# First attention's last quarter: transposes moved from TensorE to DMA, and their joins placed in the output projection

## The chip, the cores and the metric

The program runs on one core of one Trainium2 chip. The metric is the device time of one execution in microseconds, as the median of several runs.

## The reference

Two decoder layers over 256 tokens of 1024 features in float32. Layer 0 mixes tokens with a dilated sliding-window attention, layer 1 with a forgetting attention, and a gated feed-forward network follows each. What matters here is layer 0's mixer: three groups of 16 heads of 64 features (windows of dilation 1, 4 and 16), whose softmaxes are merged by their denominators, and the output projection behind it:

```python
def dilated_mixer(h, w_in, w_out):
    proj = (h @ w_in).reshape(B, S, N_GROUPS, 3, N_HEADS, HEAD_DIM)
    for g, (window, dil) in enumerate(DILATED_PATTERNS):
        q = partial_rotary(proj[:, :, g, 0], pos)
        k = partial_rotary(proj[:, :, g, 1], pos)
        v = proj[:, :, g, 2]
        o, lse = dilated_band_attention(q, k, v, dil, window // dil)
    ...
    wts = jax.nn.softmax(jnp.stack(lses, axis=0), axis=0)
    o = jnp.einsum('gbsh,gbshd->bshd', wts, jnp.stack(outs, axis=0))
    return o.reshape(B, S, ATTN_WIDTH).astype(h.dtype) @ w_out
```

## The kernel before

**Arithmetic.** Each float32 matrix product is made of three multiplications (`mm3`): operands are split into a high half (written by ScalarE, L80) and a low half (the rest, by VectorE, L84), and high x high, high x low and low x high are added in PSUM. I call the three together a product. Weights arrive in pieces of two loads of 512 KB (`raw`, five buffers, issued by SyncE at L101), and each load is split once by L80 and once by L84 into `wh` and `wl` (four buffers each). A load may be issued when the low half of the load five places earlier has been made.

**The first attention** goes over four quarters of heads (`hq` 0 to 3), each of two pairs (`pr` 0, 1) of two heads. A quarter's work is strung between the projections of the next by a table of due times (`later(i, fn, ...)`): scores, masks, softmax (`softmax_a`, in tiles `p` of 128 x 640, that is five blocks of 128 for a head), the transposing of these probabilities, and the values (`pv_a`, L313: the transposed probabilities times `v`, 24 small multiplications a pair), whose result is split into row blocks `oth`/`otl`, the input of the output projection.

The probabilities are transposed in two ways. For quarters 0 to 2, `turn_a`: GpSimd copies a head's tile so that the low 16-bit halves of all its words lie apart from the high ones (L528), a DMA issued by SyncE transposes this as ten blocks of 16-bit numbers (L530, tile `turned`), and ScalarE joins the halves again (L531). For quarter 3, `trans_a`: TensorE transposes blocks against an identity (`transposed`, L301; ten for a pair), and ScalarE and VectorE copy them out of PSUM (L306).

**The output projection** (`out_proj`) multiplies two token tiles (`t` 0, 1), with two halves of the columns (`n`) and eight row blocks (`k`): 16 products per token tile, accumulated in `ps_sc` for t = 0 and `ps_mm` for t = 1. Row blocks 6 and 7 come from quarter 3. What is still due from the attention is strung between the products of t = 0: after six products the transposes of pair 0, after three more those of pair 1, after three more the values of both pairs; then come the products of blocks 6 and 7, the residual and the norm of tile 0, and t = 1's products with the norm's transposes (L196) behind 12 of them.

**Order.** Each engine and the queue of SyncE run their instructions strictly in the order that the tile framework wrote; parts of the program under `first()` get a higher priority in it, and `tc.issue_after(x)` places instructions behind `x`. The copies of values (L285, sixteen a quarter) run on GpSimd.

Of the kernel before, what the change touches and what calls it, by code (L numbers as in the profile page):

```python
# [10 lines left out]
F32 = mybir.dt.float32  # L11
# [6 lines left out]
P = 128  # L18
D = 1024
S = 256  # L20
# [12 lines left out]
def trunk(ctx: ExitStack, tc: tile.TileContext, T, out):  # L33
# [219 lines left out]
    def p_tile(n=512, dtype=F32, name="p"):  # L253
        return ap.tile([P, 640], dtype, tag="p", name=name, bufs=6)[:, :n]

    def v_tile(o=None, r=None):

        v = ap.tile([P, 512], F32, tag="v", name="v", bufs=7)
        with first():
            if r:  # L260
                for t in range(2):
                    s = slice(t * S, (t + 1) * S)
                    nc.scalar.activation(v[:, s], o[:, s], AF.Copy, scale=r[t])
            elif o is not None:
                nc.scalar.activation(v, o, AF.Copy)
        return v
# [28 lines left out]
    copied = {}  # L295

    def transposed(blocks, copy=nc.vector.tensor_copy, tag="tr", home="pt"):

# [208 lines left out]
                    else:  # L507
                        nc.vector.tensor_scalar(s, s, f, None, op0=ALU.mult)

    def trans_a(quad, pr):  # L510

        pt = quad["pt"]
        block = lambda h, i: pt[pr, h][:, i * P:(i + 1) * P]
        home = ("pt", "bias")[pr]
        quad["w", pr] = [transposed([block(h, 1 + qb) for h in range(2) for qb in range(2)], nc.scalar.copy, home=home),
                         transposed([block(h, 3) for h in range(2)], home=home),
                         transposed([block(h, b * 4) for h in range(2) for b in range(2)], nc.scalar.copy, "o", home)]

    def turn_a(quad, pr):

        quad["w", pr] = []
        bufs = {"pt": 3, "bias": 4}
        parts = lambda x: x[:, :640].bitcast(U16).rearrange("p (c t) -> p t c", t=2)
        for h in range(2):
            home = ("pt", "bias")[pr]
            w = ap.tile([P, 640 if home == "pt" else 6 * P], F32, tag=home, name="pt", bufs=bufs[home])
            split16 = w[:, :640].bitcast(U16)
            nc.gpsimd.tensor_copy(split16.rearrange("p (t c) -> p t c", t=2), parts(quad["pt"][pr, h]))  # L528
            turned = ap.tile([P, 6 * P], F32, tag="bias", name="turned", bufs=4)[:, :640].bitcast(U16)
            nc.sync.dma_start_transpose(turned.rearrange("p (g c) -> p g c", c=P), split16)  # L530
            nc.scalar.copy(parts(w), turned.rearrange("p (t c) -> p t c", t=2))  # L531
            quad["w", pr].append(w)

    def pv_a(quad, pr):
        vs, ws = quad["v"], quad["w", pr]
        o = psum("o")
        if len(ws) == 2:
            blocks = [w[:, :640].rearrange("p (i j) -> p i j", j=P) for w in ws]
            straight = lambda h: ws[h][:, P:3 * P]
            corner = lambda h: ws[h][:, 3 * P:4 * P]  # L540
            dilated = lambda h, a: blocks[h][:, 0:5:4, a * 32:a * 32 + 32]
        else:
            straight = lambda h: ws[0][:, h * S:(h + 1) * S]
            corner = lambda h: ws[1][:, h * P:(h + 1) * P]
            dilated = lambda h, a: halves(ws[2][:, h * S:(h + 1) * S], a)
        pv(o[:, :S], vs[0], 0, pr, straight, S, True, False)
        pv(o[:, P:S], vs[0], 1, pr, corner, P, False, False)
        halves = lambda x, a: x.rearrange("p (b n) -> p b n", b=2)[:, :, a * 32:a * 32 + 32]
        for a in range(4):
            pv(halves(o[:, :S], a), vs[1 + a % 2], a // 2, pr, lambda h: dilated(h, a), 64, False, a == 3)  # L550
# [10 lines left out]
    for i, (hq, g, w) in enumerate(a_units):  # L561
# [19 lines left out]
        if w < 2:  # L581
# [26 lines left out]
            if w == 1:  # L608

                j = i + (hq == 0)  # L610
                step = lambda hq: 9 * hq + 11 + 2 * (hq == 0)
                if g == 0:
                    later(step(hq - 1) + 2 if hq else j + 3, scores_0, quad)
                if g == 2:
                    later(j + 1, scores_12, quad)
                    later(j + 1, softmax_a, quad)
                    for pr in range(2):
                        if hq == 3:
                            later(step(hq) + pr, trans_a, quad, pr)
                        else:  # L620
                            later(j + 1, turn_a, quad, pr)
                    for pr in range(2):
                        later(step(hq) + 2, pv_a, quad, pr)
        elif g == 0 and hq > 1:
# [30 lines left out]
                parts.append(sq(hn[:, s]))  # L655
        return hn, parts

    def out_proj(nm, ot, h, grow, ks, done, banks):

        ws = [weights(nm, i) for i in range(4)]  # L660
        xt = xt_tile()
        res = []

        def part(t, acc, nk):
            last = None
            for n, k in nk:
                c = (k % 2) * D + n * 512
                last = mm3(acc[n], both(ot, ALL, k, slice(t * P, (t + 1) * P)),
                           both(ws[k // 2], ALL, slice(c, c + 512)), k == 0, k == KT - 1)
            return last  # L670

        def cols(ks):
            return [(n, k) for n in range(2) for k in ks]

        for t in range(2):
            acc = [psum(banks[t]) for _ in range(2)]
            if t == 0:

                nk = cols(range(ks))
                last = part(t, acc, nk[:done])  # L680
                nk = nk[done:]
                per = -(-len(nk) // (len(due) - 1))
                for i in sorted(due):
                    with tc.issue_after(last.ins):
                        for fn, a in due[i]:
                            fn(*a)
                    last = part(t, acc, nk[:per]) or last
                    nk = nk[per:]
                due.clear()
                part(t, acc, nk)  # L690
                last = part(t, acc, cols(range(ks, KT)))
            else:
                part(t, acc, cols(range(2)))
                with tc.issue_after(last.ins):
                    part(t, acc, cols(range(2, 6)))
                    norm_t(*res[0], grow, xt, 0)
                    part(t, acc, cols(range(6, KT)))
            res.append(residual(acc, h[t], f"h_{nm}{t}"))
        return res, xt


    def ffn(l, hs, xt, grow, mid):
# [106 lines left out]
        res.append(residual(acc[1], hs[1][0], f"hf{l}1") if l == 0 else (acc[1], hs[1][0]))  # L809
        return res  # L810

    g_f = load_grow(1)
    hs, xt = out_proj("a_out", ot, x, g_f, 6, 6, ("sc", "mm"))
    cst.tile([P, P], F32, name="gap")
    bf = cst.tile([P, NH], F32, name="bf")
    nc.sync.dma_start(bf, T["bf"].partition_broadcast(P))
# [189 lines left out]
        for fn, a in due.pop(i, ()):  # L1006
            fn(*a)
    g_f = load_grow(3)
    hs, xt = out_proj("b_out", ot, [h for h, _ in hs], g_f, 6, 9, ("mm", "sc"))

    def finish(t, h, parts):
        r = rstd(parts)
# [126 lines left out]
```

## Time and profile before

| | us |
|---|---|
| median of 3 runs | 737.42 (736.22 to 738.65) |
| the profiled execution | 736.1 |
| its span, first to last instruction | 734.3 |
| TensorE busy in the span | 726.4 (99%) |
| VectorE busy | 495.9 (68%) |
| ScalarE busy | 388.7 (53%) |
| GpSimd busy | 83.0 (11%) |

The profile names engines PE (TensorE), PEld (its weight loads), DVE (VectorE), ACT (ScalarE), POOL (GpSimd) and SP (SyncE, with its DMA queue). Times in rows are microseconds from the start of the span unless marked ns. Matmuls are pipelined: how long work takes TensorE is read from one start to the next, not from a row's length. The last product of the attention's projections ends at about 225.5, and the output projection takes from there to about 253.4.

### The profile page before, as it was taken

How to read it: one execution, taken by the hardware profiler on the slowest of the kernel's cores; microseconds unless marked ns; L12 is line 12 of the kernel's file. 1: busy time of each engine (PE TensorE's matmuls, PEld its weight loads, DVE VectorE, ACT ScalarE, POOL GpSimd, SP SyncE). 2: the span in 40 equal slices, each digit the busy share in tenths (PEclk: the TensorE clock that was granted, in tenths of full speed). 3: DMA queues.
4: the chain of work that ended last, by engine and by line, in shares of the span. 5: the costliest groups of instructions: out<-in, count | busy, mean ns of one | idle time of the engine just before them, and what ended most of it. 6: DMA issues, size and time to landing. Idle time of an engine off the chain costs nothing.

```text
span 734.3 us, 14310 instructions
## 1 busy us (share of the span) xinstructions
PE 726.4 (99%) x5856; PEld 672.4 (92%) x5856; DVE 495.9 (68%) x762; ACT 388.7 (53%) x617; POOL 83.0 (11%) x118
## 2 busy tenths in 40 slices
PE   9999999999999999999999999999999999999996
PEld 7999989999988899999999989999889999999995
DVE  6997998998996775554555474576776554556533
ACT  7646747738445663444554453587475444545421
POOL 0600206007105000000000004110010000000001
PEclk9999999999999999999999999999999999999998
DMA  9865955956864376656567352874547656656601
GB/s 335 306 202 174 237 182 153 289 193 152 268 194 160 116 241 221 195 179 203 195 202 247 127 168 90 294 260 138 172 142 237 222 179 203 195 188 218 198 1 58
DMA packets 55042, 141.93 MB, mean 193 GB/s; under 512 B 20257, under 2 KB 21441, under 8 KB 54977
## 3 DMA queue, kind: packets, MB, share of 16 engines
q1 hardware_dynamic: 54832, 140.88, 59.4%
q8 instruction: 46, 0.75, 0.4%
q14 instruction: 20, 0.16, 0.1%
q10 hardware_dynamic: 144, 0.15, 0.1%
HBM read 136.00 MB, written 1.07 MB: 187 GB/s over the span
## 4 chain that ended last, share of the span: by engine, by line
PE 97%; DVE 1%; ACT 1%; POOL 0%; issue 0%; POOLq 0%; DVEq 0%; ACTq 0%
PE ps_mm L208 34%; PE ps_mm L203 17%; PE ps_tr L208 9%; PE ps_sc L208 8%; PE ps_o L208 7%; PE ps_tr L203 5%; PE ps_sc L203 4%; PE ps_o L203 4%; PE ps_o L313 2%; PE ps_sc L395 2%; PE ps_tr L196 1%; PE ps_tr L301 1%; PE ps_sc L476 1%; PE ps_o L322 1%; PE ps_sc L894 0%; PE ps_sc L458 0%
## 5 line engine op out<-in xcount | busy, mean ns | idle before, releaser
L80 ACT ACTIVATE wh<-raw 128x1024 fp32r<-128x1024 f32 x236 | 243.4, 1054 | 207.1 <-PE ps_tr L208 66.7
L84 DVE TENSOR_TENSOR wl<-raw,wh 128x1024 fp32r<-128x1024 f32 x236 | 288.3, 1242 | 82.6 <-ACT wh L80 82.4
L203 PE MATMUL ps_mm<-xt,wh 128*128 128x256 f32 x816 | 227.2, 279 | 0.2 <-ACT v L281 0.2
L208 PE MATMUL ps_mm<-xt,wl 128*128 128x256 f32 x816 | 226.0, 277 | 0.0
L208 PE MATMUL ps_mm<-xt,wh 128*128 128x256 f32 x816 | 226.0, 277 | 0.0
L203 PEld LDWEIGHTS ps_mm<-xt,wh 128*128 128x128 f32 x816 | 153.1, 188 | 2.2 <-issue 1.7
L208 PEld LDWEIGHTS ps_mm<-xt,wl 128*128 128x128 f32 x816 | 153.6, 188 | 0.1
L208 PEld LDWEIGHTS ps_mm<-xt,wh 128*128 128x128 f32 x816 | 153.4, 188 | 0.0
L208 PE MATMUL ps_tr<-xt,wh 128*128 128x256 f32 x304 | 83.9, 276 | 0.0
L208 PE MATMUL ps_tr<-xt,wl 128*128 128x256 f32 x304 | 83.9, 276 | 0.0
L203 PE MATMUL ps_tr<-xt,wh 128*128 128x256 f32 x304 | 83.7, 276 | 0.0
L730 DVE TENSOR_TENSOR sa<-ps_tr,sa 128x256 f32<-128x256 f32 x38 | 16.1, 424 | 73.5 <-PE ps_tr L208 73.5
L208 PEld LDWEIGHTS ps_tr<-xt,wh 128*128 128x128 f32 x304 | 57.1, 188 | 0.0
L208 PEld LDWEIGHTS ps_tr<-xt,wl 128*128 128x128 f32 x304 | 57.0, 188 | 0.0
L203 PEld LDWEIGHTS ps_tr<-xt,wh 128*128 128x128 f32 x304 | 57.0, 188 | 0.0
L203 PE MATMUL ps_mm<-wh,xt 128*128 128x512 f32 (+1 forms) x144 | 49.8, 346 | 0.0
L173 POOL TENSOR_SCALAR rs<-ssq 128x1 f32<-128x1 f32 x7 | 1.9, 271 | 420.6 <-ACT junk L182 420.6
L208 PE MATMUL ps_mm<-wl,xt 128*128 128x512 f32 (+1 forms) x149 | 49.1, 335 | 0.0
L208 PE MATMUL ps_mm<-wh,xt 128*128 128x512 f32 (+1 forms) x149 | 49.1, 335 | 0.0
L285 POOL COPY v<-v 32x256 f32<-32x256 f32 x64 | 40.5, 632 | 71.2 <-ACT v L281 68.6
L203 PE MATMUL ps_sc<-wh,ah 128*128 128x512 f32 x80 | 31.4, 392 | 0.0
L208 PE MATMUL ps_sc<-wl,ah 128*128 128x512 f32 (+1 forms) x82 | 31.3, 385 | 0.0
(232 smaller groups left out, 1113.6 us busy)
## 6 DMA issues: line engine op xcount, KB each, us to landing
raw<-in_gu SPq DMA_DIRECT2D x88, 512.0 KB, 4.8
raw<-in_a_in SPq DMA_DIRECT2D x68, 512.0 KB, 5.0
raw<-in_dn SPq DMA_DIRECT2D x44, 512.0 KB, 4.7
raw<-in_b_in SPq DMA_DIRECT2D x24, 512.0 KB, 5.0
raw<-in_a_out SPq DMA_DIRECT2D x8, 512.0 KB, 5.0
raw<-in_b_out SPq DMA_DIRECT2D x8, 512.0 KB, 4.4
bias<-sums SPq DMA_DIRECT2D x8, 384.0 KB, 6.6
grow<-in_norms SPq DMA_DIRECT2D x4, 512.0 KB, 5.7
```

Of the source, the lines that this page charges most:

```text
L80: a = nc.scalar.activation(view(hi), src, AF.Copy)
L84: return nc.vector.tensor_tensor(view(lo), src, view(hi).bitcast(F32), op=ALU.subtract)
L196: nc.tensor.transpose(tr[:, k * P:(k + 1) * P], xn[:, kk * P:(kk + 1) * P], ident)
L203: nc.tensor.matmul(o, sh, mh, start=start, stop=False)
L208: last = nc.tensor.matmul(o[:, u], s, m[:, u], start=False, stop=end and u.stop == n)
L285: nc.gpsimd.tensor_copy(v[1 + a % 2][n:n + 32, a // 2 * S:a // 2 * S + S], by_t[a * 32:a * 32 + 32, t, g])
L301: nc.tensor.transpose(tr[:, i * P:(i + 1) * P], b, ident)
L313: nc.tensor.matmul(o[h * HD:(h + 1) * HD], v[:, c:c + HD], w(h), start=start, stop=stop)
L322: nc.tensor.matmul(o[:, :n], mhalf.to_broadcast([P, P]), mhalf.to_broadcast([P, n]), start=True, stop=True)
L395: nc.tensor.matmul(lead[t], xt[y][:, k, t * P:(t + 1) * P], w[z][:, u], start=k + y + z == 0, stop=k == KT - 1 and z == 1)
L476: nc.tensor.matmul(sc[h][c, o:o + 64], q[HR[h], pr, qb * P + a * 32:qb * P + a * 32 + 32], k[HR[h], pr].rearrange("p (b n) -> p b n", b=2) ...
L730: nc.vector.tensor_tensor(a, u, sg, op=ALU.mult)
```

## The change

The quarter 3 of the first attention also goes through `turn_a`. Its parting copies run on GpSimd for pair 0 and on VectorE for pair 1, under `first()`. The joins are taken out of `turn_a` into `join_a`; for quarter 3 they are due at 38 and 39, in the output projection, with `tc.issue_after` the last copy of values of that quarter's own head group (`copied["v"]`, L263 before), on ScalarE for pair 0 and on VectorE for pair 1. The turned tiles get another home: for the first head of pair 1 the buffers `pt`, else `bias`. `out_proj` takes an explicit list of products that come before and between the due work: eight products of t = 0 (blocks 0 to 3), four of t = 1 (blocks 0 and 1), four of t = 0 (blocks 4 and 5), with the due work behind the fourth, the ninth and the sixteenth. The second layer's output projection passes a list that gives the same order as before.

```diff
-    def trans_a(quad, pr):
...
+    def parted(x):
+        return x.bitcast(U16).rearrange("p (c t) -> p t c", t=2)
 
     def turn_a(quad, pr):
 
-        quad["w", pr] = []
-        bufs = {"pt": 3, "bias": 4}
-        parts = lambda x: x[:, :640].bitcast(U16).rearrange("p (c t) -> p t c", t=2)
+        last = quad["hq"] == 3
+        by = (nc.gpsimd, nc.vector)[last and pr].tensor_copy
+        home = lambda tag: ap.tile([P, 640 if tag == "pt" else 6 * P], F32, tag=tag, name="pt",
+                                   bufs={"pt": 3, "bias": 4}[tag])[:, :640]
+        quad["w", pr], quad["turned", pr] = [], []
         for h in range(2):
...
-            nc.gpsimd.tensor_copy(split16.rearrange("p (t c) -> p t c", t=2), parts(quad["pt"][pr, h]))
-            turned = ap.tile([P, 6 * P], F32, tag="bias", name="turned", bufs=4)[:, :640].bitcast(U16)
-            nc.sync.dma_start_transpose(turned.rearrange("p (g c) -> p g c", c=P), split16)
-            nc.scalar.copy(parts(w), turned.rearrange("p (t c) -> p t c", t=2))
+            with first() if last else nullcontext():
+                w = home(("pt", "bias")[pr])
+                apart = w.bitcast(U16)
+                by(apart.rearrange("p (t c) -> p t c", t=2), parted(quad["pt"][pr, h]))
+                turned = home(("bias", "pt")[pr * (h == 0)]).bitcast(U16)
+                nc.sync.dma_start_transpose(turned.rearrange("p (g c) -> p g c", c=P), apart)
             quad["w", pr].append(w)
+            quad["turned", pr].append(turned)
+            if not last:
+                join_a(quad, pr, h)
+
+    def join_a(quad, pr, h, by=nc.scalar.copy):
+        with tc.issue_after(copied["v"].ins) if quad["hq"] == 3 else nullcontext():
+            by(parted(quad["w", pr][h]), quad["turned", pr][h].rearrange("p (t c) -> p t c", t=2))
...
-                        if hq == 3:
-                            later(step(hq) + pr, trans_a, quad, pr)
-                        else:
-                            later(j + 1, turn_a, quad, pr)
+                        later(j + 1, turn_a, quad, pr)
+                        for h in range(2) if hq == 3 else ():
+                            later(38 + pr, join_a, quad, pr, h, (nc.scalar.copy, nc.vector.tensor_copy)[pr])
...
-    def out_proj(nm, ot, h, grow, ks, done, banks):
+    def out_proj(nm, ot, h, grow, head, at, banks):
...
+        cols = lambda t, ks: [(t, n, k) for n in range(2) for k in ks]
+        last = None
+        for a, b in zip((0, *at), (*at, len(head))):
+            last = part(head[a:b]) or last
+            if due:
                 with tc.issue_after(last.ins):
-                    part(t, acc, cols(range(2, 6)))
-                    norm_t(*res[0], grow, xt, 0)
-                    part(t, acc, cols(range(6, KT)))
-            res.append(residual(acc, h[t], f"h_{nm}{t}"))
+                    for fn, a in due.pop(min(due)):
+                        fn(*a)
+        last = part(cols(0, range(KT)))
+        res = [residual(accs[0], h[0], f"h_{nm}0")]
+        part(cols(1, range(2)))
+        with tc.issue_after(last.ins):
+            part(cols(1, range(2, 6)))
+            norm_t(*res[0], grow, xt, 0)
+            part(cols(1, range(KT)))
+        res.append(residual(accs[1], h[1], f"h_{nm}1"))
         return res, xt
...
-    hs, xt = out_proj("a_out", ot, x, g_f, 6, 6, ("sc", "mm"))
+    hs, xt = out_proj("a_out", ot, x, g_f, blocks(0, range(2)) + blocks(1, range(1)) + blocks(0, (2,)), (4, 9, 16),
+                      ("sc", "mm"))
```

In the queue of SyncE, from the loads of the output weights (`in_a_out`) to those of the first gate weights (`in_gu`) and first `in_dn` load (the line numbers are those of each kernel; `pt<-pt` is now the name of what was `turned<-pt`):

```order
 L101 DMA raw<-in_a_out 128x1024 x8
-L101 DMA raw<-in_gu 128x1024 x8
+L101 DMA raw<-in_gu 128x1024
+L526 DMA_TRANSPOSE pt<-pt 128x10x128 x2
+L101 DMA raw<-in_gu 128x1024
+L526 DMA_TRANSPOSE pt<-pt 128x10x128
+L101 DMA raw<-in_gu 128x1024 x2
+L526 DMA_TRANSPOSE pt<-pt 128x10x128
+L101 DMA raw<-in_gu 128x1024 x4
 L101 DMA raw<-in_dn 128x1024 x2
```

Four transposing DMAs now stand among the eight loads, the last one behind four of them.

On VectorE, from the last scaling of probabilities of quarter 3 (`p<-p,c`) to the low halves of the values (`otl<-ps_o,oth`); `wl<-raw,wh` are low halves of weights, L524 the parting copies and L534 the joins of pair 1:

```order
 L508 TENSOR_SCALAR p<-p,c 128x384
-L84 TENSOR_TENSOR wl<-raw,wh 128x1024 x4
-L306 COPY pt<-ps_tr 128x256 x2
+L84 TENSOR_TENSOR wl<-raw,wh 128x1024
+L524 COPY pt<-p 128x1280 x2
+L84 TENSOR_TENSOR wl<-raw,wh 128x1024 x3
+L534 COPY pt<-pt 128x2x640 x2
+L84 TENSOR_TENSOR wl<-raw,wh 128x1024 x2
 L84 TENSOR_TENSOR otl<-ps_o,oth 128x2x4x32 x2
```

The first four low halves here are of the output weights (pieces five to eight of the eight loads); the two that now follow the joins are of the first gate weights, and stood behind the norm of tile 0 before.

## Rows read from the trace of the kernel before

**Rows 1.** Page: busy time by engine, and the chain that ended last.

```profile
PE 726.4 (99%) x5856; PEld 672.4 (92%) x5856; DVE 495.9 (68%) x762; ACT 388.7 (53%) x617; POOL 83.0 (11%) x118
...
PE 97%; DVE 1%; ACT 1%; POOL 0%; issue 0%; POOLq 0%; DVEq 0%; ACTq 0%
```

**Rows 2.** Timeline of PE, output projection: start, length, instruction, count.

```profile
225.52 0.40 PE L203 MATMUL ps_sc<-wh,oth 128*128 128x512 f32 x1
...
229.63 0.81 PE L301 MATMUL ps_tr<-ident,p 128*128 128x128 f32 x6
...
231.43 0.39 PE L203 MATMUL ps_sc<-wh,oth 128*128 128x512 f32 x1
...
236.09 2.45 PE L313 MATMUL ps_o<-pt,v 128*64 128x256 f32 x48
238.47 0.50 PE L203 MATMUL ps_sc<-wh,oth 128*128 128x512 f32 x1
...
239.05 0.39 PE L208 MATMUL ps_sc<-wh,otl 128*128 128x512 f32 x1
239.28 0.50 PE L203 MATMUL ps_sc<-wh,oth 128*128 128x512 f32 x1
...
240.28 0.40 PE L203 MATMUL ps_sc<-wh,oth 128*128 128x512 f32 x1
```

**Rows 3.** Timeline of DVE: a low half of the values; idle before in brackets.

```profile
238.15 0.62 DVE L84 TENSOR_TENSOR otl<-ps_o,oth 128x256 fp32r<-128x256 f32 x1 [4.05 <-ACT oth L80]
```

**Rows 4.** POOL: L285's busy time in a window; L528's durations (ns, min/median/max).

```profile
219.60:224.85 5.25, 4.81 (x9) 1.00 0.55 204
...
L528 POOL COPY pt<-p x12: 1247/1358/2245, 72.2 to 183.4; 128x1280 uint16<-128x1280 uint16 x12
```

**Rows 5.** Timelines of DVE and POOL: low halves of weights; scalings and a parting copy.

```profile
225.41 5.41 DVE L84 TENSOR_TENSOR wl<-raw,wh 128x1024 fp32r<-128x1024 f32 x4
...
245.73 2.35 DVE L84 TENSOR_TENSOR wl<-raw,wh 128x1024 fp32r<-128x1024 f32 x2
...
167.75 0.35 DVE L508 TENSOR_SCALAR p<-p,c 128x256 f32<-128x256 f32 x1
...
168.02 0.41 DVE L508 TENSOR_SCALAR p<-p,c 128x384 f32<-128x384 f32 x1
...
168.48 1.34 POOL L528 COPY pt<-p 128x1280 uint16<-128x1280 uint16 x1 [38.70 <-DVE p L508]
...
168.62 1.41 DVE L508 TENSOR_SCALAR p<-p,c 128x384 f32<-128x384 f32 x1
```

**Rows 6.** SP's queue and its transposing DMAs (twelve; the one at 80.80), ScalarE's joins.

```profile
226.84 0.33 SPq L101 DMA_DIRECT2D raw<-in_gu  x1
...
L530 SPq DMA_TRANSPOSE turned<-pt x12: 1267/1366/1601, 73.8 to 185.0; - x12
...
DMA to landing us min/median/max: 3.3/3.5/5.8
...
78.58 1.46 SPq L101 DMA_DIRECT2D raw<-in_a_in  x2
80.80 1.60 SPq L530 DMA_TRANSPOSE turned<-pt  x1
...
DMA to landing us min/median/max: 5.4/5.4/5.4
...
L531 ACT COPY pt<-turned x12: 1647/1672/1698, 77.5 to 188.5; 128x1280 uint16<-128x1280 uint16 x12
```

**Rows 7.** Timelines of DVE and PE: the norm of tile 0 and its transposes.

```profile
244.40 1.42 DVE L191 SCALAR_TENSOR_TENSOR xn<-h_a_out,rs,grow 128x512 f32<-128x512 f32 x2 [0.69 <-POOL rs L176]
...
249.83 1.04 PE L196 MATMUL ps_tr<-ident,xn 128*128 128x128 f32 x8
```

**Rows 8.** Windows: length, busy us of PE, PEld, DVE, ACT, POOL; granted clock; DMA.

```profile
225.00:250.00 25.00, 25.00 (x161) 20.31 (x160) 13.35 (x17) 11.53 (x19) 7.02 (x9) 1.00 0.33 105
730.10:734.00 3.90, 0.00 (x0) 0.00 (x0) 0.67 (x2) 0.48 (x1) 0.00 (x0) 0.50 0.38 134
```

More of the change, by code (lines that the diff above doesn't have):

```diff
@@ L508, in softmax_a @@
                         nc.vector.tensor_scalar(s, s, f, None, op0=ALU.mult)
-    def trans_a(quad, pr):
[L512 to L517, printed above, removed]
@@ L536, in pv_a @@
         o = psum("o")
[L537 to L541, printed above, removed]
[L542 to L547 removed]
+        blocks = [w.rearrange("p (i j) -> p i j", j=P) for w in ws]
+        pv(o[:, :S], vs[0], 0, pr, lambda h: ws[h][:, P:3 * P], S, True, False)
+        pv(o[:, P:S], vs[0], 1, pr, lambda h: ws[h][:, 3 * P:4 * P], P, False, False)
         halves = lambda x, a: x.rearrange("p (b n) -> p b n", b=2)[:, :, a * 32:a * 32 + 32]
         for a in range(4):
[L550 removed]
+            pv(halves(o[:, :S], a), vs[1 + a % 2], a // 2, pr, lambda h: blocks[h][:, 0:5:4, a * 32:a * 32 + 32],
+               64, False, a == 3)
         src = o[:, :S].rearrange("p (b a u) -> p b a u", b=2, a=4)
@@ L656, in residual, with part @@
         return hn, parts
-    def out_proj(nm, ot, h, grow, ks, done, banks):
+    def out_proj(nm, ot, h, grow, head, at, banks):
         ws = [weights(nm, i) for i in range(4)]
         xt = xt_tile()
-        res = []
-        def part(t, acc, nk):
+        accs = {}
+        done = set()
+        def part(items):
             last = None
-            for n, k in nk:
+            for t, n, k in items:
+                if (t, n, k) in done:
+                    continue
+                done.add((t, n, k))
+                if t not in accs:
+                    accs[t] = [psum(banks[t]) for _ in range(2)]
@@ L667, in part @@
                 c = (k % 2) * D + n * 512
-                last = mm3(acc[n], both(ot, ALL, k, slice(t * P, (t + 1) * P)),
+                last = mm3(accs[t][n], both(ot, ALL, k, slice(t * P, (t + 1) * P)),
                            both(ws[k // 2], ALL, slice(c, c + 512)), k == 0, k == KT - 1)
             return last
[L672 to L693, printed above, removed]
-                with tc.issue_after(last.ins):
-                    part(t, acc, cols(range(2, 6)))
-                    norm_t(*res[0], grow, xt, 0)
-                    part(t, acc, cols(range(6, KT)))
-            res.append(residual(acc, h[t], f"h_{nm}{t}"))
@@ L810, in ffn, with blocks @@
         return res
+    def blocks(t, ks):
+        return [(t, n, k) for i in ks for n in range(2) for k in (2 * i, 2 * i + 1)]
     g_f = load_grow(1)
-    hs, xt = out_proj("a_out", ot, x, g_f, 6, 6, ("sc", "mm"))
+    hs, xt = out_proj("a_out", ot, x, g_f, blocks(0, range(2)) + blocks(1, range(1)) + blocks(0, (2,)), (4, 9, 16),
+                      ("sc", "mm"))
     cst.tile([P, P], F32, name="gap")
@@ L1008, in trunk @@
     g_f = load_grow(3)
-    hs, xt = out_proj("b_out", ot, [h for h, _ in hs], g_f, 6, 9, ("mm", "sc"))
+    hs, xt = out_proj("b_out", ot, [h for h, _ in hs], g_f, [(0, n, k) for n in range(2) for k in range(6)], (9, 12),
+                      ("mm", "sc"))
     def finish(t, h, parts):
```

8 lines of the change are left out of this document (2 added, 6 removed).

## The prediction, made before the changed kernel ran

> **What bounds the kernel now.** I read the shares of the engines first and then the chain of work that ended last: TensorE is busy 99% of the span and holds 97% of the chain [rows 1]. So a microsecond counts only if TensorE has less to do, or has to wait. Next I read TensorE's timeline through the output projection of the first attention [rows 2]. One product there (three multiplications of 128x512) takes (229.63 - 225.52) / 6 = 0.685 us. From 229.63 to 231.43 stand ten transposes and one product: 1.80 - 0.685 = 1.115 us for the ten, and the same again for the second pair of heads three products later. The last values (48 small multiplications) run from 236.09 to 238.47. Behind them the products of the last two row blocks need what the values gave: ScalarE makes their high halves and VectorE, behind it, the low halves (0.62 us each) [rows 3]. The first such product starts its third multiplication, which needs the low half, at 239.05, and the second product takes 240.28 - 239.28 = 1.00 us where 0.685 is usual: 0.31 us of waiting that is there already.
>
> **What goes.** Twenty transposes: 2 x 1.115 = 2.23 us of TensorE's own time. The six copies out of PSUM (four on ScalarE, two on VectorE) go too; both engines have idle time there and TensorE waits for neither, so I count nothing. Sixteen products now stand ahead of the values and four fewer behind them: nothing in the sum, since all of them run in any case. Without any wait the values would then start at 225.52 + 16 x 0.685 = 236.48, about where they start now, end at 238.86, and the third multiplication of the first product behind them would start 0.58 us later, at 239.44.
>
> **What comes, and whether it is ready.** In place of each pair's transposes stand, for each of two heads, a copy that parts the 16-bit halves, a transposing DMA, and a copy that joins them. The kernel does this already for three quarters of the heads, so its prices are in the trace [rows 4, 6]. What differs is the place: here the values wait for it soon after. I follow it in time, all as an estimate from rows.
>
> GpSimd. The order puts the two parting copies of pair 0 behind nine of the sixteen copies of values. Nine end at 224.85 [rows 4]. A parting copy takes 1.25 to 1.36 us alone. [...]
>
> VectorE. The low half of the fifth piece of the output weights runs at 227.7 to 228.8 instead of ending at 226.8. Then come the two parting copies of pair 1. The trace has no such copy on VectorE. Its scalings of 256 and 384 columns take 0.35 and 0.41 us, which carried on to 1280 columns gives 0.41 + 896 x 0.06 / 128 = 0.83 us; ScalarE takes 1.67 us for the same shape [rows 5, 6]. I take 0.85, the value from VectorE's own SBUF-to-SBUF rows, and keep 0.83 to 1.67. With a copy of values let in between, they end at about 231.1; the low halves of the sixth and seventh pieces follow, 1.14 us each alone and 1.33 beside GpSimd [rows 5], and end at about 232.3 and 233.6.
>
> The queue of SyncE. It goes strictly in order, and a load of the next weights waits until the low half that frees its buffer is done: now the load at 226.84 is issued right behind the low half that starts at 225.41 [rows 5, 6]. In the new order stand: turn, turn, load, turn, load, load, turn. Turns one and two go out at 226.2 and 227.7 (1.37 us of issue each), the load at 229.1, turn three at about 229.8, the next load only at 232.3, the one behind it only at 233.6, and **turn four at 234.0**. Turn four also waits for the first join, since its target is the buffer that this join reads; that is done by about 231.6, ahead of the load. Twelve turns landed 3.3 to 5.8 us after issue, 3.5 in the middle. The one at 80.80, with two loads right in front of it as here, took 5.4 [rows 6]. I take 5.4, as this row is nearest, and keep 3.4 to 5.8.
>
> So turn four lands at 239.4. The join of it, on VectorE, ends at 240.25, and only then can the values of pair 1 run; pair 0's could run on time, since ScalarE's joins end at about 233.3. That would cost some 2.6 us (values of pair 1 at 240.25 instead of 237.67). But the new order on VectorE has two low halves of gate weights behind the joins and **ahead of** the low halves of the values: 2 x 1.14 = 2.3 us more, then 0.62 [rows 3, 5]. The third multiplication of the first product behind the values can start at 240.25 + 2.3 + 0.62 = 243.17 instead of 239.44: 3.7 us of waiting, inside which the 2.6 lies. The later 0.31 us of waiting goes, as both low halves then follow each other.
>
> Behind that, the norm's transposes now stand behind 8 products instead of 12, 5.5 us after the last row-block product. Today this product ends at about 241.7 and the normed row is ready at 245.82 [rows 7], 4.1 us later, with the same instructions between; 1.4 us are left, so no wait. The turned buffers of the first three quarters get other homes, which takes a wait from GpSimd there; TensorE has none there to lose, so nothing.
>
> **Sum**, against the profiled execution (736.1 us, of which 734.3 are the span): -2.23 - 0.31 + 3.7 = +1.2 us, so 737.3. That execution lies 1.3 below the median of the runs (737.42), so I predict **738.6** on the scale of the median. With turn four landing in 3.4 us the wait is 1.7: 736.6 on the same scale. With 5.8, and VectorE's copies at 1.67 (which moves turn four to about 234.3 as well), it is 5.2: +2.7, so 740.1.
>
> [...]
>
> **Rivals.** (1) The latency is hidden and the gain stays. Then the time falls by 2.2 us, or 2.5 if the old wait goes too: 734.9 to 735.2. It needs turn four to land by 239.44 - 0.62 - 2.3 - 0.85 = 235.7, so to be issued by 232.2 even at 3.4 us. [...] Chance 0.19.
> (2) Slower: VectorE's four added copies run at one element a cycle (1.5 to 1.67 us each). Their place is on the chain to turn four and again in the last join; price +2.3 to +2.9 over the median, 739.7 to 740.3. It decides from a third multiplication at about 244.2 on. For it: ScalarE's price for the shape; against it: VectorE's own rows. Chance 0.20.
> (3) Slower: TensorE, left idle for most of 3.7 us, is granted its lower clock. [...] No wait near 3 us stands in this trace in the middle of work, and the stall here comes in two parts with multiplications between. Chance 0.04. [...]
> (4) The change doesn't do what it says: the joins could sit elsewhere in the queues than behind the copy of the last values. The order shows them there, behind two high halves on ScalarE; 0.02, at 737.4.
>
> **How the numbers follow.** The forecast, part of the wait exposed, has 0.55. About 0.3% (2.2 us) is what a measurement of this kernel can tell from no change: 735.2 to 739.6. Of the forecast's own range (736.6 to 739.6) all lies inside it. Rival 1 straddles the lower bound: 0.14 faster, 0.05 within. Rival 2 lies beyond the upper one: 0.18 slower, 0.02 within; rival 3 is slower, rival 4 within. So faster 0.14, within 0.64, slower 0.22. The range takes in the forecast and rival 2 and leaves out rival 3 and most of rival 1 (together under 0.2): 735.4 to 740.4.
>
> **What would show it.** In the profile of the changed kernel: L301's transposes gone in the output projection; the last turn issued behind two loads near 234 and landing near 239; the join on VectorE right behind that; the second half of L313's values starting near 240 rather than 237.7; the low halves of the values behind two low halves of gate weights, and TensorE waiting for them. Wrong at the root would be values that run through from 236.5 to 238.9 (then rival 1), a parting copy on VectorE of 1.5 us (rival 2), a granted clock under 1.00 between 238 and 260 (rival 3), or TensorE waiting for GpSimd's copies of values at 236.5.

## The result, and the profile of the changed kernel

The changed kernel takes **739.79 us** (median of 17 runs, 737.40 to 743.11) against 736.31 us of the kernel before, run beside it (17 runs, 734.40 to 738.65). The ratio is **1.0048, 95% interval 1.0037 to 1.0058**: slower by 3.5 us, beyond the 0.3% that the prediction set as the border of "within". The time lies inside the range on record (735.4 to 740.4), but not where the likeliest case had it. On the scale of the new median of before that case stands at 736.31 + 1.2 = 737.5 us, 2.3 us short, and of the three outcomes that the prediction named, "slower" had a chance of 0.22.

The profiled execution takes 741.1 us, of which 739.2 are the span (before: 736.1 and 734.3). First the page: the shares of the engines and the chain that ended last.

```profile
PE 727.5 (98%) x5836; PEld 671.8 (91%) x5836; DVE 503.0 (68%) x764; ACT 389.5 (53%) x615; POOL 88.4 (12%) x120
...
PE 85%; DVE 6%; DMA 4%; ACT 3%; issue 1%; SPq 0%; POOL 0%; POOLq 0%; DVEq 0%; ACTq 0%
```

TensorE still bounds, but it is no longer the whole chain as in [rows 1]: 12% of the last chain has left it, mostly to VectorE and to DMA. Where it leaves is in the list of TensorE's waits (what waited, for whom, us):

```profile
PE ps_o L313 <- DVE pt L534: 2.7, 1, 2.7
PE ps_o L322 <- DVE mhalf L66: 0.9, 1, 0.9
PE ps_mm L203 <- DVE qk L443: 0.6, 1, 0.6
PE ps_sc L395 <- ACT wh L80: 0.3, 1, 0.3
```

The second wait is the start of the program, which the kernel before has too. The fourth lies in the second layer and is no more than the small waits that come and go from trace to trace. The other two are new, and they lie 160 us apart. The first is the stall that the prediction forecast. The third is in quarter 0 of the attention, where the prediction had counted nothing.

**The forecast stall.** TensorE's timeline behind the sixteen products (start, length, instruction, count, in brackets the idle time before it and its releaser), to be held against [rows 2]:

```profile
239.72 0.60 PE L313 MATMUL ps_o<-pt,v 128*64 128x256 f32 x2
243.02 1.53 PE L313 MATMUL ps_o<-pt,v 128*64 128x256 f32 x22 [2.71 <-DVE pt L534]
244.49 0.80 PE L203 MATMUL ps_sc<-wh,oth 128*128 128x512 f32 x1
...
245.78 0.79 PE L208 MATMUL ps_sc<-wh,otl 128*128 128x512 f32 x1
246.37 0.63 PE L203 MATMUL ps_sc<-wh,oth 128*128 128x512 f32 x1
...
247.54 0.39 PE L203 MATMUL ps_sc<-wh,oth 128*128 128x512 f32 x1
```

The transposes are gone. The values of pair 0 run on time, and so do two multiplications of pair 1; the other 22 wait 2.71 us for the join on VectorE. And the products behind them are slow: from 244.49 to 247.54 stand six multiplications, 3.05 us, where six take 1.37 us in [rows 2] (0.685 us for three). The windows (length, busy us of PE, PEld, DVE, ACT, POOL; then the granted clock, the DMA share and GB/s) show the clock that goes with it:

```profile
240.00:243.00 3.00, 0.31 (x2) 0.00 (x0) 0.91 (x2) 0.55 (x1) 0.00 (x0) 1.00 0.85 250
243.00:244.50 1.50, 1.48 (x23) 1.29 (x23) 1.50 (x2) 0.00 (x0) 0.00 (x0) 0.83 0.00 0
244.50:246.00 1.50, 1.42 (x4) 0.70 (x4) 1.50 (x3) 0.65 (x1) 0.00 (x0) 0.50 0.40 131
246.00:247.50 1.50, 1.50 (x4) 1.21 (x5) 0.24 (x1) 0.00 (x0) 0.00 (x0) 0.54 0.86 270
247.50:248.90 1.40, 1.40 (x7) 1.13 (x7) 0.69 (x1) 0.43 (x1) 0.00 (x0) 1.00 0.70 246
```

The granted clock is 0.50 to 0.54 for some 3 us behind the stall and back at 1.00 after it. In the kernel before it is 1.00 through the whole stretch [rows 8].

Behind the stall stands the last turn. SyncE's queue and VectorE's timeline, to be held against [rows 5, 6]:

```profile
227.64 3.62 SPq L526 DMA_TRANSPOSE pt<-pt  x2
231.37 0.70 SPq L101 DMA_DIRECT2D raw<-in_gu  x1
232.17 1.35 SPq L526 DMA_TRANSPOSE pt<-pt  x1
233.61 1.30 SPq L101 DMA_DIRECT2D raw<-in_gu  x2
235.02 1.94 SPq L526 DMA_TRANSPOSE pt<-pt  x1
```

```profile
227.76 2.27 DVE L84 TENSOR_TENSOR wl<-raw,wh 128x1024 fp32r<-128x1024 f32 x1
229.95 1.95 DVE L524 COPY pt<-p 128x1280 uint16<-128x1280 uint16 x2
...
237.45 0.90 DVE L534 COPY pt<-pt 128x1280 uint16<-128x1280 uint16 x1 [1.55 <-DMA pt<-pt]
242.09 0.88 DVE L534 COPY pt<-pt 128x1280 uint16<-128x1280 uint16 x1 [3.74 <-DMA pt<-pt]
242.86 2.35 DVE L84 TENSOR_TENSOR wl<-raw,wh 128x1024 fp32r<-128x1024 f32 x2
245.13 1.12 DVE L84 TENSOR_TENSOR otl<-ps_o,oth 128x256 fp32r<-128x256 f32 x2
```

The order in the queue is the forecast one: turn, turn, load, turn, load, load, turn. The time from issue to landing of the last turn, by its line:

```profile
DMA to landing us min/median/max: 7.0/7.0/7.0
```

It lands at 242.0, and VectorE's join follows at once. In the four kernels whose queue has this order (the changed one, `q0_home_back`, `gates_behind` and `four_ahead`) the last turn lands 6.8 to 7.4 us after its issue.

**The shift ahead of it.** Matching the multiplications of the two traces one by one, the changed kernel is 0.4 us late from the first 20 us on (a difference that starts where the two programs are alike), 1.3 us late behind the wait at 81 us, and 1.8 to 2.0 us late from 98 us until the output projection. That projection adds 2.7 us more (4.55 late at the fifth product of t = 1), and only 0.3 us follow to the end.

### The profile page after: what moved, and what is told of

Read it like the earlier page. It is cut to its first block, busy times and chain, and to the rows that moved or that the text cites. A ratio compares the mean times of both kernels' runs of the same rounds, so it can differ in the third digit from the quotient of the medians.

```text
span 739.2 us, 14281 instructions
## 1 busy us (share of the span) xinstructions
PE 727.5 (98%) x5836; PEld 671.8 (91%) x5836; DVE 503.0 (68%) x764; ACT 389.5 (53%) x615; POOL 88.4 (12%) x120
## 4 chain that ended last, share of the span: by engine, by line
PE 85%; DVE 6%; DMA 4%; ACT 3%; issue 1%; SPq 0%; POOL 0%; POOLq 0%; DVEq 0%; ACTq 0%
PE ps_mm L208 29%; PE ps_mm L203 15%; PE ps_tr L208 9%; PE ps_sc L208 8%; PE ps_o L208 7%; PE ps_tr L203 5%; PE ps_sc L203 4%; PE ps_o L203 4%; DVE wl L84 2%; DMA raw<-in_b_in 2%; PE ps_o L313 1%; DMA otl<-in_lead 1%; ACT wh L80 1%; DMA pt<-pt 1%; PE ps_tr L196 1%
## 5 line engine op out<-in xcount | busy, mean ns | idle before, releaser
L84 DVE TENSOR_TENSOR wl<-raw,wh 128x1024 fp32r<-128x1024 f32 x236 | 291.8, 1257 | 79.2 <-ACT wh L80 78.8
L208 PE MATMUL ps_mm<-xt,wh 128*128 128x256 f32 x816 | 226.2, 277 | 0.0
L287 POOL COPY v<-v 32x256 f32<-32x256 f32 x64 | 43.0, 672 | 73.4 <-ACT v L283 70.7
```

Source lines behind the costliest of these rows:

```text
L84: return nc.vector.tensor_tensor(view(lo), src, view(hi).bitcast(F32), op=ALU.subtract)
L208: last = nc.tensor.matmul(o[:, u], s, m[:, u], start=False, stop=end and u.stop == n)
L287: nc.gpsimd.tensor_copy(v[1 + a % 2][n:n + 32, a // 2 * S:a // 2 * S + S], by_t[a * 32:a * 32 + 32, t, g])
```

## The experiments

All times are medians; the ratio is to the kernel before in the same session (its medians there: 735.57 to 736.31 us). All of them at a glance, then each with what it was for.

| kernel | us | ratio (95%) |
|---|---|---|
| changed kernel | 739.79 | 1.0048 (1.0037 to 1.0058) |
| homes_alone | 737.38 | 1.0017 (1.0007 to 1.0027) |
| homes_q12 | 735.92 | 0.9997 (0.9987 to 1.0008) |
| tensor_both | 737.27 | 1.0012 (1.0003 to 1.0021) |
| one_pair | 735.59 | 1.0000 (0.9989 to 1.0010) |
| turn4_first | 735.36 | 0.9992 (0.9979 to 1.0004) |
| turn4_first_q0 | 734.75 | 0.9983 (0.9973 to 0.9993) |
| turn4_first_q0_gates | 734.65 | 0.9983 (0.9973 to 0.9993) |
| warm | 738.93 | 1.0042 (1.0026 to 1.0057) |
| gates_behind | 740.29 | 1.0067 (1.0053 to 1.0081) |
| four_ahead | 741.65 | 1.0065 (1.0043 to 1.0087) |
| four_ahead_gates | 737.62 | 1.0028 (1.0017 to 1.0039) |
| q0_home_back | 740.91 | 1.0057 (1.0038 to 1.0076) |

### 1. The new homes of the first three quarters

`homes_alone`: the kernel before, and of the change only this:

```
-turned = ap.tile([P, 6 * P], F32, tag="bias", name="turned", bufs=4)[:, :640].bitcast(U16)
+t_home = ("bias", "pt")[pr * (h == 0)]
+turned = ap.tile([P, 640 if t_home == "pt" else 6 * P], F32, tag=t_home, name="turned", bufs=bufs[t_home])[:, :640].bitcast(U16)
```

> The kernel before with one thing of the change: the new homes of the turned tiles in quarters 0 to 2 (a tile of the probabilities' ring where pair 1, head 0 is turned). Theory A: this alone makes TensorE wait near 81 us. GpSimd's fourth parting copy starts some 2 us earlier (at 77.3 instead of 79.2), meets a low half of weights on VectorE that then takes 2.27 us instead of 1.21, and the product that needs PSUM back waits 0.6 us; with the slower rhythm of the products behind it (118 ns instead of 113 from one multiplication to the next) the shift is 1.5 us. Then the time is 0.8 to 1.5 us above the kernel before: 737.1 to 737.8. Theory B (the prediction's: the new homes cost nothing, and the shift at 81 us belongs to one execution): 736.3, and no wait of TensorE at 81 us.

It takes 737.38 us, 1.1 us more than the kernel before (interval 0.5 to 2.0), and its trace has the wait of 0.6 us. `homes_q12` is the same with `pr * (h == 0) * (quad["hq"] > 0)`, so quarter 0 keeps its old home:

> The kernel before with the new homes of the turned tiles in quarters 1 and 2 only; quarter 0 keeps its old one. Theory A (the cost of the homes, 1.1 us in homes_alone, is the collision of quarter 0 near 81 us): no wait of TensorE there, and the time of the kernel before, 736.2 (735.7 to 736.7). Theory B (the cost lies in the other quarters, or in no single place): 737.4 as homes_alone.

It takes the time of the kernel before (735.92 against 736.07 beside it), and the wait is not in its trace. So the cost is that of **quarter 0**. The traces agree, product by product: between 80.5 and 82 us TensorE falls 0.86 to 0.89 us behind the kernel before in all nine kernels with quarter 0's new home, and not at all (0.01 us or less) in the four with the old one. The mechanism is in the timelines of GpSimd and VectorE; first the kernel before, then the changed one:

```profile
79.21 1.56 POOL L528 COPY pt<-p 128x1280 uint16<-128x1280 uint16 x1 [2.64 <-ACT pt L531]
...
77.31 2.35 DVE L84 TENSOR_TENSOR wl<-raw,wh 128x1024 fp32r<-128x1024 f32 x2
...
79.59 0.74 DVE L442 STREAM_SHUFFLE rt<-ps_mm 128x512 f32<-128x512 f32 x1
80.23 0.66 DVE L443 TENSOR_TENSOR qk<-ps_mm,rcos 128x512 f32<-128x512 f32 x1
```

```profile
77.25 1.65 POOL L524 COPY pt<-p 128x1280 uint16<-128x1280 uint16 x1 [0.28 <-DVE p L508]
...
77.71 3.40 DVE L84 TENSOR_TENSOR wl<-raw,wh 128x1024 fp32r<-128x1024 f32 x2
...
81.04 0.73 DVE L442 STREAM_SHUFFLE rt<-ps_mm 128x512 f32<-128x512 f32 x1
81.67 0.67 DVE L443 TENSOR_TENSOR qk<-ps_mm,rcos 128x512 f32<-128x512 f32 x1
```

Before, GpSimd's fourth parting copy waits 2.64 us for a join to free its buffer, and so runs beside the operations of lines 442 and 443 on VectorE: they take 0.74 and 0.66 us there, and 0.73 and 0.67 us in the changed kernel, where that copy has ended before them. With the new home it starts at 77.25, beside a low half, and the two low halves take 3.40 us instead of 2.35. The product that needs the PSUM back from line 443 waits (0.6 us in the list of waits). So beside this copy the low halves, which read `raw` and `wh`, took 1.05 us more, and lines 442 and 443, which read `ps_mm`, nothing. Why the one is held up and the others are not was not shown.

`q0_home_back` does the same to the changed kernel, and its time did not fall:

> The changed kernel with the turned tiles of quarter 0 back in their old home. Theory A (the new home costs at 81 us): 0.8 to 1.5 us under the changed kernel, 738.3 to 739.0, no wait of TensorE at 81 us. Theory B: as the changed kernel, 739.8.

It takes 740.91 us, not 738.3 to 739.0. The wait at 81 us is gone from its trace, but TensorE still waits 2.8 us for the last join, and the granted clock falls there too (0.75 from 238 to 243, 0.91 from 243 to 248). Its six executions lie between 737.9 and 742.0 us, the profiled one the lowest of them: with the stall in the kernel, this experiment can't show a difference of 1 us. I asked again without the stall, in `turn4_first_q0` (below): 734.75 against 735.36, with ratios that differ by 0.0009. That is the expected sign, and the size (0.6 us) is not told apart from none. For the homes the times to go by are those of the pair `homes_alone` and `homes_q12`.

### 2. The last turn behind the loads

`turn4_first`: the first load stays where it is, the next three are issued behind the last turn. On the other four engines the order stays word for word the same. Of the edit this is the line that does it; the others name the last turn (`copied["turn"]`) and let the program ask for these loads later.

```
...
+with tc.issue_after(copied["turn"].ins) if key[0] == "gu0" and (key[1], c) in ((0, 1), (1, 0), (1, 1)) else nullcontext():
     nc.sync.dma_start(raw, T[key[0]][key[1]][:, u])
...
```

> The changed kernel with three loads of the next weights moved behind the last turn in the queue of SyncE; nothing else moves on any engine. Theory A: the last turn goes out right behind the third, near 233.5 instead of 235.0, lands after 3.5 to 5.4 us as most turns do (237 to 239 instead of 242.0), its join ends by 238 to 240, the second half of the values runs without a wait or with at most 0.5 us of one, and TensorE's granted clock stays at 1.00 behind it. Then 2.7 us of wait and 1.6 us of lower clock go: 735.3 to 736.5. Theory B: it lands 7 us after its issue whatever stands in front of it, at 240.5; then only 1.5 us of the wait goes, 737.5 to 738.3.

735.36 us, **4.4 us under the changed kernel** and level with the kernel before (0.9992, 0.9979 to 1.0004). Theory A holds. SyncE's queue:

```profile
227.15 6.88 SPq L527 DMA_TRANSPOSE pt<-pt  x4
234.07 6.87 SPq L104 DMA_DIRECT2D raw<-in_gu  x6
```

The landings of these four turns, by their line, then TensorE's timeline and windows:

```profile
DMA to landing us min/median/max: 3.4/3.6/3.7
```

```profile
237.80 2.45 PE L314 MATMUL ps_o<-pt,v 128*64 128x256 f32 x48
240.18 0.50 PE L206 MATMUL ps_sc<-wh,oth 128*128 128x512 f32 x1
...
241.16 0.50 PE L211 MATMUL ps_sc<-wh,otl 128*128 128x512 f32 x1 [0.24 <-DVE otl L86]
```

```profile
238.00:243.00 5.00, 4.76 (x58) 3.67 (x55) 3.41 (x5) 2.24 (x3) 0.00 (x0) 1.00 1.02 379
243.00:248.00 5.00, 5.00 (x24) 4.14 (x23) 2.41 (x5) 1.61 (x5) 0.80 (x2) 1.00 0.27 110
```

The last turn lands 3.4 us after its issue instead of 7.0, the 48 multiplications of the values run in one piece (2.45 us, as in [rows 2]), and the granted clock stays at 1.00 from 225 to 252. So the stall and what follows it are worth 4.1 to 4.4 us, more than the 2.7 us that TensorE stands idle.

`tensor_both` gives the other end: the new homes and the new order of products, but both pairs transposed on TensorE. `one_pair` has only pair 1 there, and pair 0 turned by DMA.

> The changed kernel with its new homes and its new order of products, but both pairs of the last quarter transposed on TensorE as before: no parting copy, turn or join there. Theory A (the order costs nothing, the homes cost 1.1 us as homes_alone showed): 737.4 (736.9 to 737.9). Theory B (the order itself costs, since four products fewer stand behind the values and the norm comes sooner): 738.2 or more. Either way its distance to turn4_first is what the transposing DMAs of the last quarter are worth once they are hidden; the prediction's terms say 2.2 to 2.5 us.

> The changed kernel with pair 0 alone turned by DMA; pair 1 is transposed on TensorE, in front of the tenth product, and its two parting copies, two turns and two joins are gone. Theory A (the loss sits in the last two turns, behind the loads): ScalarE's joins of pair 0 end some 3 us ahead of the values, no wait of TensorE there, and ten transposes (1.1 us) saved against tensor_both (737.4): 736.3 (735.8 to 736.8). Theory B (parting and joining cost TensorE something whichever pair they serve, by holding VectorE up): 737.4 or more.

737.27 us for `tensor_both` is what `homes_alone` takes: **the order of products costs nothing** that these times can tell (their intervals are about 1 us to either side). To `turn4_first` it is 0.0020 of the ratio, 1.5 us (0.3 to 2.6, with the two intervals taken as independent), and in the traces 2.2 us: from 222 us to the fifth product of t = 1 `turn4_first` gains 2.1 us on the kernel before, `tensor_both` loses 0.1. The prediction's 2.23 us for the transposes stands. `one_pair` takes 735.59 us: 1.7 us less than `tensor_both` by the median (0.9 by the ratio) where 1.1 was expected, with no new wait in the output projection. So the loss sits in pair 1's turns and not in parting and joining as such.

### 3. The clock

`warm` puts 24 multiplications that nobody reads between the values of pair 0 and pair 1:

```
+if quad["hq"] == 3 and pr:
+    idle = psum("tr")
+    for i in range(24):
+        nc.tensor.matmul(idle[:, :S], ot[0][:, i % 4, :P], ot[0][:, i % 4, :], start=True, stop=True)
```

> The changed kernel with 24 multiplications of 128x256 that nobody reads (0.113 us each, 2.7 us) put between the values of pair 0 and those of pair 1, where TensorE waits 2.7 us. Theory A: behind the wait the clock falls to half because TensorE was idle; six multiplications of 128x512 take 3.05 us there instead of 1.39. With the wait filled the clock stays at 1.00, and the kernel gets faster by work added: 739.8 - 1.6 = 738.2. Theory B: the slow multiplications are slow for what they read, not for the idleness: 739.8 or up to 0.5 more.

738.93 us is 0.9 us under the changed kernel, but the intervals of the ratios overlap: the expected sign, at half the size, and not settled by the times alone. The trace settles what the multiplications read: TensorE's timeline, then the windows behind the stall with the granted clock.

```profile
239.11 3.12 PE L541 MATMUL ps_tr<-oth 128*128 128x256 f32 x24
...
244.00 1.33 PE L313 MATMUL ps_o<-pt,v 128*64 128x256 f32 x22 [1.19 <-DVE pt L534]
245.25 0.50 PE L203 MATMUL ps_sc<-wh,oth 128*128 128x512 f32 x1
...
246.75 0.51 PE L208 MATMUL ps_sc<-wh,otl 128*128 128x512 f32 x1 [0.76 <-DVE otl L84]
247.09 0.39 PE L203 MATMUL ps_sc<-wh,oth 128*128 128x512 f32 x1
```

```profile
244.50:246.00 1.50, 1.49 (x20) 0.98 (x17) 1.50 (x2) 0.63 (x1) 0.00 (x0) 1.00 0.00 0
246.00:247.50 1.50, 0.75 (x3) 0.66 (x4) 1.21 (x3) 0.00 (x0) 0.00 (x0) 1.00 0.79 262
```

The same multiplications on the same operands now run at their usual pace with the clock at 1.00 (0.23 us from one start to the next from 247.09 on; in the changed kernel 3.05 / 6 = 0.51): they were slow for the clock and not for what they read. Part of the gain is given back at once: with the clock up, TensorE reaches the low halves 0.76 us before they are ready.

The mean granted clock of every execution shows how often the clock falls. In the kernels without the stall of some 3 us, and in `warm`, it is 0.997 to 0.999 in every execution. In the kernels with it, it is 0.996 or less in 11 of 17 (changed kernel), 6 of 6 (`q0_home_back`), 5 of 6 (`gates_behind`) and 4 of 6 (`four_ahead`). The eleven of the changed kernel have a median of 740.3 us, the other six 738.7: 1.6 us apart. That is a split made after the fact and no experiment, but it says what a single trace can't: the lower clock is the usual case here, not the accident of one execution.

### 4. The low halves of gate weights

`gates_behind` moves the two low halves of gate weights behind those of the values (their `issue_after` is the last `otl`) and nothing else on any engine but VectorE.

> The changed kernel (739.8) with one thing moved: the two low halves of gate weights that stood on VectorE behind the last join and ahead of the low halves of the values now stand behind these. The prediction's working gave them 2.3 us of the wait: then 737.5. Theory from the trace of the changed kernel: they end at 245.21, while the values of pair 1 themselves end on TensorE at 244.5 and their high half on ScalarE at 245.24, so that at most 0.2 to 0.6 us hang on them as long as the join is as late as it is: 739.2 to 739.6.

740.29 us: no gain that the times show. Even the part of the prediction's wait that hangs on these two alone, 3.7 - 2.6 = 1.1 us, is not there. The values of pair 1 need some 1.3 to 1.5 us after the join and their high half 0.6 us more, and the two low halves run in that time. The term isn't nothing, though: the low half of pair 0's values, which could be made at once, stands behind them too, and where the clock stays up (`warm`) TensorE waits 0.76 us for it. In the profiled execution of the changed kernel, with the clock at 0.50 there, the list of waits has none for it.

Where the mechanism bites harder showed in a failed attempt to give the last turn more time. `four_ahead` adds `blocks(1, (1,))` to the head, four more products in front of the values:

> The changed kernel with four more products of the second half of the tokens ahead of the last values (20 instead of 16), so that the last values come 2.75 us later and the last turn has that much more time. Theory A: the wait of 2.7 us is gone and with it the lower clock (1.6 us); of the cover behind the values four products are lost, and the norm's transposes, which now have some 4.1 us between the last product of the first half and the normed row but only four products (2.75 us) to fill it, wait 1.4 us. Sum 739.8 - 2.7 - 1.6 + 1.4 = 736.9 (736.0 to 737.5). Theory B: the join lands later too, because what is queued is queued by TensorE's pace, and the wait stays: 739.8 or more.

741.65 us, 1.9 more than the changed kernel by the medians and 1.3 by the ratios, whose intervals overlap; the gain that was expected isn't there. The wait for the join is indeed down to 0.2 us; a new one stands behind it. VectorE, then TensorE:

```profile
243.86 4.62 DVE L84 TENSOR_TENSOR wl<-raw,wh 128x1024 fp32r<-128x1024 f32 x4
248.40 1.11 DVE L84 TENSOR_TENSOR otl<-ps_o,oth 128x256 fp32r<-128x256 f32 x2
```

```profile
249.05 0.51 PE L208 MATMUL ps_sc<-wh,otl 128*128 128x512 f32 x1 [2.57 <-DVE otl L84]
```

The four products free a second piece of output weights early, so two more low halves of gate weights are put ahead of the values'. `four_ahead_gates` puts all of them behind; with that the norm's transposes move too, from behind four products to behind seven or eight:

> The kernel four_ahead (741.7) with the low halves of the gate weights put behind the low halves of the values on VectorE. Theory A: the four products that four_ahead puts in front free the second piece of output weights sooner, so four low halves of gate weights instead of two slip in ahead of the values' low halves, and the 2.6 us for which TensorE waits there are theirs. Then 741.7 - 2.6 = 739.1 or a little less (738.0 to 739.5), with the wait for the join (0.2) and for the normed row (0.7 or more, as low halves now run among the additions that lead to it) left. Theory B: TensorE waits there for the values themselves, whatever stands in front: 741.7.

737.62 us, 4.0 under `four_ahead` by the medians (expected 2.2 to 3.7) and 2.7 by the ratios, and that wait is gone; what is left is 1.2 us for the join and 0.2 us for the normed row (0.7 in `four_ahead`). So low halves of weights in front of the low halves of the values do cost: four of them 2.57 us of waiting, two at most 0.8 (`warm`), since these run largely under the values.

### 5. All together

`turn4_first_q0` is `turn4_first` with quarter 0's old home, and `turn4_first_q0_gates` has the low halves of the gate weights behind as well.

> The changed kernel with the loads behind the last turn, as in turn4_first (735.4), and with the turned tiles of quarter 0 in their old home. Theory A (the new home costs where quarter 0 is turned; it was hidden in q0_home_back by the spread of the stall that is gone here): no wait of TensorE at 81 us and 0.6 to 1.4 us under turn4_first, 734.0 to 734.8. Theory B (it costs nothing in the end): 735.4.

> The kernel turn4_first_q0 (734.75) with the two low halves of gate weights behind the low halves of the values. Its trace shows TensorE waiting 0.5 us for the low halves of the values; that wait goes: 734.2 (733.8 to 734.6). If instead the low halves, now among the additions behind the output projection, hold the normed row up by 2.4 us, 0.9 us more than the 1.5 us it has to spare, it is 735.2.

734.75 and 734.65 us, both 0.9983 (0.9973 to 0.9993): **faster than the kernel before by about 1.2 us**, and some 5 us under the changed kernel. The last step removes the wait of 0.5 us from the trace and nothing that the times can tell.

## Why the prediction was right and wrong

- *Twenty transposes, 2.23 us, and the new order of products for nothing.* Right: `tensor_both` against `homes_alone` and `turn4_first`.
- *VectorE's copies at 0.85 us.* Right, if a little low: 1.95 us for the two parting copies, 0.90 and 0.88 for the joins. Rival 2 falls: 0.88 us is about half of ScalarE's 1.67 for the shape [rows 6].
- *The last turn behind two loads, and the values of pair 1 some 2.6 us late.* Right in place and near in size: 2.71 us of idle time. Two errors cancel in part. With the 1.9 us of shift ahead taken off, the turn goes out at 235.0 - 1.9 = 233.1, not 234.0; and it lands 7.0 us after issue, not 5.4, so 0.7 us later in all. Counted as the prediction counts, from start to start, the values end 3.6 us late (244.49 instead of 238.55 + 2.38) where 2.6 was forecast. The range of 3.4 to 5.8 for that landing, from twelve turns of the kernel before, was too narrow: none of those had three loads and a turn in flight in front of it. `turn4_first` shows the cause, since without the three loads it is 3.4. The start of that chain, turns one and two at 226.2 and 227.7 and the low half of the fifth piece at 227.7 to 228.8, was an estimate, and no run shows it as it stands: in the changed kernel these turns go out at 227.64 and 229.03, and that low half starts at 227.76 and takes 2.27 us, beside GpSimd's two parting copies (226.37 to 228.94).
- *Two low halves of gate weights ahead of the values' low halves: the rest of the 3.7 us, 1.1.* Too much: `gates_behind` gains nothing that the times show, and where the clock stays up the wait is 0.76 us (`warm`). The sum put them one after the other behind the join and let the values' own 1.3 us and the high half's 0.6 us pass for nothing.
- *Rival 3, the lower clock, at 0.04.* Mis-sized. Against it the prediction set that the stall comes in two parts with multiplications between. In the profiled execution six multiplications take 3.05 us instead of 1.37, 1.7 us more; the values around the stall take 244.49 - 238.55 - 2.71 = 3.2 us instead of 2.4. Of these 0.85 us, 0.21 are the lower clock's, since the 22 multiplications behind the wait take 244.49 - 243.02 = 1.47 us here and 244.45 - 243.19 = 1.26 in `gates_behind`, with the clock at 1.00; the other 0.64 come with the break itself. Of the 1.7 us, some 0.8 would have been a wait for the low halves had the clock stayed up (`warm`). It was never as far as all twelve products behind the stall at half the clock, which would be 12 x 0.685 = 8.2 us more. With the clock in the sum, this stretch adds up: -2.54 + 2.71 + 1.68 + 0.85 = +2.7 us, what the two traces differ by there. The step that failed is the reason given against the rival, that multiplications between the two parts of the stall would keep the clock up: by the mean clock it fell in 11 of 17 executions.
- *The new homes of the first three quarters, "nothing".* Wrong, and the other main error: +1.1 us by the times (`homes_alone`, `homes_q12`), 0.87 us in the traces. The step followed the wait that goes away on GpSimd and stopped there. That VectorE is held up beside a parting copy was in [rows 5] (a scaling of 1.41 us instead of 0.41), and 150 us later the forecast has a low half run late; where the copy *moves to*, and what of VectorE's it meets there, was not asked.
- *The norm's transposes don't wait.* Right: no wait of that kind in the changed kernel. `four_ahead`, with four products fewer behind the values, does wait 0.7 us for the normed row.
- *The copy of values on GpSimd in time, the change doing what it says.* Right: the last of these copies ends at 236.59 in the changed kernel, and the values start at 238.55.

So the stall, which was the argument of the prediction, came as forecast, and the result is slower by more than that for the two terms set at zero, clock and homes. The size of the clock's share stays open within bounds: undoing the stall gives back 4.1 to 4.4 us, of which 2.7 are idle time and 0.6 the break in the values; `warm` gains 0.9, and the executions at the higher mean clock lie 1.6 us lower than the others.

That the time lies inside the range on record is luck. The upper end of that range was set for rival 2, VectorE's slow copies, which did not come; two other terms, priced at or near nothing, took the time there.

## What to carry to other kernels

A DMA whose landing is waited for should go into its queue ahead of loads that nobody needs soon: on an engine-bound path the place of three loads decided over 4 us, and the change from loss to gain. When an edit takes away a wait, follow the freed instruction to the place where it now runs and see what it meets there; the wait may have kept two engines apart. And price a stall of the engine that bounds with what its clock does afterwards (here 0.50 to 0.54 for some 3 us in the profiled execution), not only with the idle time.

## What the runs showed of the hardware that I had not expected

**A stall of about 3 us lowers the clock in one execution and not in another.** In the changed kernel's trace 2.71 us of waiting are followed by some 3 us at 0.50 to 0.54. In that of `gates_behind` the wait is longer, and the clock stays (timeline of TensorE, then the window behind the wait):

```profile
243.19 1.33 PE L314 MATMUL ps_o<-pt,v 128*64 128x256 f32 x22 [3.16 <-DVE pt L535]
```

```profile
244.50:246.00 1.50, 1.50 (x7) 0.85 (x7) 0.79 (x2) 0.62 (x1) 0.00 (x0) 1.00 0.00 0
```

That execution (739.15 us, mean clock 0.997) is the lowest of its six, whose median is 740.29; the other five have 0.994 or 0.995. In `four_ahead` the clock stays at 1.00 behind 2.57 us as well. So one profile tells neither that a stall is harmless to the clock nor what it costs on the median; the mean clock of every execution does tell how often it falls.

**A steady run of multiplications has two rhythms.** The projections' multiplications of 128x256 between 83 and 97 us, durations in ns (min/median/max), first in the kernel before, then in the changed one, both at a granted clock of 1.00:

```profile
L208 PE MATMUL ps_mm<-xt,wh x42: 276/276/276, 82.8 to 96.7; 128*128 128x256 f32 x42
```

```profile
L208 PE MATMUL ps_mm<-xt,wh x40: 281/281/282, 83.0 to 96.8; 128*128 128x256 f32 x40
```

From one start to the next it is 113 ns in the one and 118 in the other, over some 140 multiplications: the 0.6 to 0.7 us by which the shift grows from 82 to 98 us. In these traces the rhythm is taken up where the stream starts anew and kept until it breaks; what sets it stays open. It is not tied to the wait (`homes_alone` has the wait at 81 us and 276 ns behind it), and the kernel before has the slower rhythm elsewhere (115 to 143 us). It makes differences of 0.5 to 1 us between two traces that no edit explains, so shifts of that size are to be judged by repeated runs.
